# The mixers' small transfers issued by GpSimd instead of SyncE

## The chip, the cores and the metric

The kernel runs on one core of one Trainium2 chip. The metric is the time of one execution in microseconds (us); the median of several runs counts. The engines have short names in what follows: PE is TensorE (matmuls), DVE is VectorE, ACT is ScalarE, POOL is GpSimd and SP is SyncE. SP computes nothing here, it only issues transfers (DMAs). POOL computes and, in this kernel, already issues a few transfers of its own. Each engine works through its own list of instructions strictly in order: an instruction that waits holds back all that stand behind it on that engine.

## The reference

One transformer block over 256 tokens of width 2048, in float32. A norm and one wide projection feed two mixers, a gated delta rule with eight heads and block attention with eight heads. Their outputs go through `w_out`, then 32 experts follow (two of them per token), and a last norm. The part that the change touches is the delta rule's inner matrices:

```python
def gdn_mixer(q, k, v, z, b, a, conv_w, A_log, dt_bias, out_norm_w):
    qkv = jax.nn.silu(causal_depthwise_conv(jnp.concatenate([q, k, v], axis=-1), conv_w))
    ...
    qh = l2norm(heads(q)) * (HEAD_DIM ** -0.5)
    kh = l2norm(heads(k))
    ...
def gated_delta_rule_chunked(q, k, v, g, beta):
    ...
    decay = jnp.exp(jnp.where(causal, g[..., :, None] - g[..., None, :], NEG_INF))
    kb = k * beta[..., None]
    L = jnp.where(strict, jnp.einsum('bhnid,bhnjd->bhnij', kb, k) * decay, 0.0)
    ...
    sol = lax.linalg.triangular_solve(eye + L, rhs, left_side=True, lower=True)
    u, w = sol[..., :Dv], sol[..., Dv:]
    attn = jnp.where(causal, jnp.einsum('bhnid,bhnjd->bhnij', q, k) * decay, 0.0)
```

## The kernel before

**Stages.** The first stage multiplies the normed tokens by `w_in`, 512 columns at a time. Such a block of columns has 16 units; a unit is one slice of 128 rows, whose weights are split into a high part `w_hi` (ACT, line 206) and a low part `w_lo` (DVE, line 208), and 6 or 12 matmuls. SP fetches the weights two units at a time into four buffers (`w_raw`, line 201), and the split runs five units ahead of the matmuls (`SPB = 6` ring tiles). Blocks come in a fixed order: `gk gq gv gz mv` for the first half of the heads, then `gk gq gv mk mq mk gz mq mv`, then four blocks of `w_out`. The second stage is the experts: eight quads of four experts, whose weights SP streams (about 400 MB, line 935) as buffers come free.

**Order of the work.** Everything in the first stage stands in an order written out by hand: the program is a loop over units, and between units a small planner (`tick`, `side_step`) lets generators advance by one step, so the mixers' work is laid between the units. What an engine executes, and in which order, is fixed when the kernel is built; only the waits decide the times. So each transfer stands at one place in its issuing engine's list, and moving it to another engine puts it at the place that the loop had reached on that engine.

**The small transfers.** Heads are done in two halves of four. For each half:

- `decay_task` (once) writes the decay rows to DRAM (`drow`, line 379); `decay` reads them back, each row copied to all 128 partitions, as `E`: two transfers per head (lines 391 and 393, 256 and 128 KB), eight per half. POOL masks them (line 400, four selects per head) and ACT takes exponentials (lines 405 to 407).
- `qk_task` computes the norm factors: POOL takes the power (line 467), PE transposes (470), ACT copies (`rks`, 472), then `drk` goes to DRAM (475) and comes back on all partitions as `RN` (479, four times 256 KB). POOL multiplies `kq` by `RN` (482), and PE forms the products `pA` (488, 493).
- `pA` times `E` goes to DRAM (`dU`, 496) and comes back as blocks of 32 by 32 (`UB`, 515). `inverse` solves them on DVE (lines 520 to 526), sends the inverses to DRAM (`dY`, 529), and `heads` fetches them as `YY` (536). Each head's first matmul on them is `pz` (line 600).

In the kernel before, SP issues all of these, between the weight loads.

Of the kernel before, what the change touches and what calls it, by code (L numbers as in the profile page):

```python
# [40 lines left out]
def bcast_rows(ap, offset, n, parts=128):  # L41
    return bass.AP(tensor=ap.tensor, offset=ap.offset + offset, ap=[[0, parts], [1, n]])
# [3 lines left out]
def tile_block(ctx, tc, x, norm_mix_w, w_in, conv_w, A_log, dt_bias, gonw, monw, w_out, nfw,  # L46
               w_rg, b_rg, w_re, b_re, w_g, w_u, w_d, nfinal, out, dbg=None):
    nc = tc.nc
# [234 lines left out]
    def more_consts():  # L283
        nc.gpsimd.iota(iot, pattern=[[1, SL]], base=1, channel_multiplier=0, allow_small_or_imprecise_dtypes=True)
        nc.gpsimd.iota(dsc, pattern=[[-1, 32]], base=32, channel_multiplier=0, allow_small_or_imprecise_dtypes=True)
        nc.vector.tensor_scalar(tri_le, di, 0.0, None, op0=OP.is_ge)
        nc.vector.tensor_scalar(tri_gt, di, 0.0, None, op0=OP.is_lt)
        nc.vector.tensor_scalar(stri_bf, di, 0.0, None, op0=OP.is_gt)
        nc.vector.memset(ones_bf, 1.0)
        yield  # L290

        dd = wt("cd", [128, 384], "E", EB)
        for c, bs in ((0, 0), (1, 128), (2, 0)):
            nc.gpsimd.iota(dd[:, c * 128:(c + 1) * 128], pattern=[[-1, 128]], base=bs, channel_multiplier=1,
                           allow_small_or_imprecise_dtypes=True)
        for c, bs in ((0, 0), (1, 128), (2, 0)):
            nc.gpsimd.affine_select(out=NEGD[:, c * 128:(c + 1) * 128], in_=dd[:, c * 128:(c + 1) * 128],
                                    pattern=[[-1, 128]], compare_op=OP.is_ge, fill=BIG, base=bs, channel_multiplier=1)
        yield
        nc.vector.tensor_mul(wr, wr, nfr[:, :, None].to_broadcast([128, NK, 36]))  # L300
        yield

        zr = wt("zr", [128, 516], "E", EB)
        nc.vector.memset(zr, 0.0)
        ones = wt("o32", [128, 8, 32], "E", EB)
        nc.vector.memset(ones, 1.0)
        yield
        for i in range(2):
            nc.sync.dma_start(dY.rearrange("c f -> (c f)").rearrange("(a p f) -> p a f", p=128, f=516)[:, i], zr)
        for g in range(4):  # L310
            ps = slice(32 * g, 32 * g + 32)
            nc.gpsimd.affine_select(out=idc[ps], in_=ones[ps], pattern=[[-1, 8], [1, 32]], compare_op=OP.is_equal,
                                    fill=0.0, base=-8 * g, channel_multiplier=0)
# [6 lines left out]
    def decay_task():  # L320
# [55 lines left out]
        rsb = prc.tile([32, 128], F32, name="rsb")  # L376
        nc.scalar.copy(rsb, pr[:32, 0:128])
        yield
        nc.sync.dma_start(drow.rearrange("a h b t -> (a h b) t"), rsb)
        push(decay(0), 3)  # L380

    E = {}
# [1 line left out]
    def decay(hf):  # L384

        heads = range(4 * hf, 4 * hf + 4)
        for H in heads:
            e = wt("E", [128, 6, 128], "E", EB)
            E[H] = e
            off = drow.offset + H * 256  # L390
            nc.sync.dma_start(e[:, 0:4].rearrange("p (a b) t -> p a (b t)", a=2),
                              bass.AP(tensor=drow.tensor, offset=off, ap=[[0, 128], [2048, 2], [1, 256]]))
            nc.sync.dma_start(e[:, 4:6],
                              bass.AP(tensor=drow.tensor, offset=off + 128, ap=[[0, 128], [2048, 2], [1, 128]]))
            yield 1
        yield 1
        for H in heads:
            e = E[H]
            for s, op in ((0, OP.is_gt), (2, OP.is_ge), (4, OP.is_gt), (5, OP.is_ge)):
                nc.gpsimd.affine_select(out=e[:, s], in_=e[:, s], pattern=[[1, 128]], compare_op=op, fill=-BIG, base=0,  # L400
                                        channel_multiplier=-1)
            yield 1
        for H in heads:
            e = E[H]
            nc.scalar.activation(e[:, 0:4:2], e[:, 0:4:2], AF.Exp, bias=negG[:, 0, H:H + 1])
            nc.scalar.activation(e[:, 1:4:2], e[:, 1:4:2], AF.Exp, bias=suf[:, H:H + 1])
            nc.scalar.activation(e[:, 4:6], e[:, 4:6], AF.Exp, bias=negG[:, 1, H:H + 1])
            if H % 2:
                yield 1
# [26 lines left out]
    def qk_task(hf, la, pb):  # L436
# [35 lines left out]
        nc.scalar.copy(rks, prk[:16, 0:128])  # L472
        yield
        drk = drp.tile([16, 128], F32, name=f"drk{hf}")
        nc.sync.dma_start(drk, rks)
        yield
        RN = [wt("RN", [128, 2, T], "YY", 4) for _ in range(4)]
        for h in range(4):
            nc.sync.dma_start(RN[h].rearrange("p a t -> p (a t)"), bcast_rows(drk, h * 512, 512))
        yield  # L480
        for h in range(4):
            nc.gpsimd.tensor_mul(kq[4 * hf + h], kq[4 * hf + h], RN[h])
# [1 line left out]
        for h in range(4):  # L484
            H = 4 * hf + h
            e = E[H]
            p0 = ps_tmp("pA0")
            nc.tensor.matmul(p0, kq[H][:, 0, 0:128], kq[H].rearrange("p a t -> p (a t)"), start=True, stop=True)
            e0 = e[:, 0:4].rearrange("p s t -> p (s t)")
            nc.vector.tensor_mul(e0, p0, e0)  # L490
            p1 = ps_tmp("pA1")
            p1v = p1[:, 0:256].rearrange("p (a t) -> p a t", a=2)
            nc.tensor.matmul(p1v, kq[H][:, 0, 128:256], kq[H][:, :, 128:256], start=True, stop=True)
            nc.vector.tensor_mul(e[:, 4:6], p1v, e[:, 4:6])
            yield 1
            nc.sync.dma_start(square(dU[hf], h), e[:, 0:5:4])
        yield
        side.append(inverse(hf))

# [10 lines left out]
    def inverse(hf):  # L510


        UB = wt("UB", [128, 32, 32], "nat", NATB)
        for g in range(4):
            nc.sync.dma_start(UB[32 * g:32 * g + 32], blocks(dU[hf], 0, 32))
        YB = wt("YB", [128, 8, 32], "YB", 1)
        nc.vector.tensor_copy(YB, idc)
        for _ in range(6):
            yield
        nc.vector.memset(UB.rearrange("p j k -> p (j k)")[:, 0:1024:33], -1.0)  # L520
        for j in range(30, -1, -1):
            n = 32 - j
            pr = wt("ybp", [128, 8, 32], "ybp", 1)[:, :, 0:n]
            nc.vector.tensor_tensor(pr, UB[:, j, None, j:32].to_broadcast([128, 8, n]), YB[:, :, j:32], op=OP.mult)
            yield
            nc.vector.tensor_reduce(YB[:, :, j:j + 1], pr, axis=AX.X, op=OP.add, negate=True)
            yield
        for g in range(4):
            nc.sync.dma_start(blocks(dY, 8 * 128 * g, 8), YB[32 * g:32 * g + 32])
        push(heads(hf), 3)  # L530

    def heads(hf):
        for h in range(4):
            y = wt("YY", [128, 2, 2, 128], "YY", 4)
            YY[4 * hf + h] = y
            nc.sync.dma_start(y[:, 1], square(dY, h))
            push(head_task(4 * hf + h), 5)
            yield 1

# [3 lines left out]
    def square(t, h):  # L543
        return bass.AP(tensor=t.tensor, offset=t.offset + 2 * h * BS, ap=[[128, 128], [BS, 2], [1, 128]])
# [242 lines left out]
    for n in range(16 * 14):  # L787
        kind, hf = chunks[n // 16]
# [617 lines left out]
```

## Time and profile before

| | us |
|---|---|
| median of three runs | 1465.89 (1465.54 to 1466.2) |
| the profiled execution, its own time | 1465.37 |
| its span, first to last instruction | 1463.6 |
| PE busy in the span | 1392.8 |
| DVE, ACT, POOL busy | 623.4, 415.0, 59.8 |

The span is what the profiler records between the first and the last instruction; the execution's own time lies 1.8 us above it. A busy PE is not PE at its peak, since matmuls overlap and their ends are modelled. Waiting, branching and issuing transfers don't count as busy. Of the DMA queues, the one that SP feeds (`q1`) moved 491.93 MB and the one that POOL feeds (`q0`) 0.20 MB.

### The profile page before, as it was taken

What the parts mean: (1) busy time and instruction counts of PE and PEld (TensorE: products, weight loads), DVE (VectorE), ACT (ScalarE), POOL (GpSimd) and SP (SyncE); (2) the same over time, 40 slices, a digit from 0 to 9 for tenths busy, and PEclk for the clock granted to TensorE, in tenths of its full rate; (3) what the DMA queues carried; (4) which work ended last, traced back from release to release, by engine and by line L of the source; (5) the groups of instructions that cost most, each with busy time, mean ns of one, the idle gap of its engine ahead of it and who ended that gap; (6) DMA issues with size and microseconds to landing.
All of it is one profiled execution on the core that took longest, in us unless ns stands there. A gap on an engine that the chain in (4) does not pass through costs nothing.

```text
span 1463.6 us, 19050 instructions
## 1 busy us (share of the span) xinstructions
PE 1392.8 (95%) x7490; PEld 809.9 (55%) x7490; DVE 623.4 (43%) x1287; ACT 415.0 (28%) x806; POOL 59.8 (4%) x93
## 2 busy tenths in 40 slices
PE   8989999999999999999999999999999899899995
PEld 8966999898888844443443443433443334234332
DVE  6846977597655442331331331331151132025024
ACT  5554445555654321120120120111130111003013
POOL 2021003100000000000000000000000000000010
PEclk9999999999999999999999999999999999999998
DMA  8557656765499579999999999999999999999993
GB/s 247 171 167 193 188 174 159 211 182 163 144 359 373 195 285 424 425 419 426 425 414 425 426 426 425 426 424 425 427 427 422 425 425 425 427 426 425 424 403 106
DMA packets 106479, 493.40 MB, mean 337 GB/s; under 512 B 22912, under 2 KB 33248, under 8 KB 77072
## 3 DMA queue, kind: packets, MB, share of 16 engines
q1 hardware_dynamic: 106080, 491.93, 86.5%
q8 instruction: 61, 1.00, 0.3%
q0 software_dynamic: 304, 0.20, 0.1%
q14 instruction: 34, 0.28, 0.1%
HBM read 488.12 MB, written 3.97 MB: 336 GB/s over the span
## 4 chain that ended last, share of the span: by engine, by line
PE 76%; DMA 10%; DVE 5%; issue 4%; ACT 3%; SPq 0%; POOL 0%; ACTq 0%; DVEq 0%; POOLq 0%
PE py L1316 15%; PE pup L1057 13%; PE pgate L1057 12%; PE pj L227 5%; PE pj L228 5%; PE pj L231 5%; DMA we<-in_w_expert_up_dram 4%; PE pj L238 4%; PE pj L241 3%; PE pj L239 3%; PE ph L1046 3%; DMA we<-in_w_expert_down_dram 2%; DMA wm<-in_w_expert_up_dram 2%; DVE acc L1305 2%; ACT xh L1029 2%
## 5 line engine op out<-in xcount | busy, mean ns | idle before, releaser
L208 DVE TENSOR_TENSOR w_lo<-w_raw,w_hi 128x512 fp32r<-128x512 f32 x288 | 197.1, 700 | 115.4 <-ACT w_hi L206 109.4
L206 ACT CAST w_hi<-w_raw 128x512 fp32r<-128x512 f32 x288 | 170.3, 619 | 108.4 <-DMA w_raw<-in_w_in_dram 57.8
L1057 PE MATMUL pup<-we,hT 128*64 128x512 f32 x608 | 165.1, 604 | 7.2 <-DMA we<-in_w_expert_up_dram 7.0
L227 PE MATMUL pj<-xth,w_hi 128*128 128x256 f32 x640 | 165.9, 293 | 0.0
L1316 PE MATMUL py<-we,hgT 128*64 128x512 f32 x544 | 162.9, 597 | 2.1 <-DMA we<-in_w_expert_down_dram 1.4
L228 PE MATMUL pj<-xtl,w_hi 128*128 128x256 f32 x640 | 158.5, 281 | 0.0
L1057 PE MATMUL pgate<-we,hT 128*64 128x512 f32 x528 | 149.1, 600 | 0.0
L227 PEld LDWEIGHTS pj<-xth,w_hi 128*128 128x128 f32 x640 | 121.5, 190 | 1.9 <-ACT w_hi L206 0.4
L228 PEld LDWEIGHTS pj<-xtl,w_hi 128*128 128x128 f32 x640 | 121.8, 190 | 0.2
L1300 DVE SCALAR_TENSOR_TENSOR yl<-py,sl,yh 128x512 fp32r<-128x512 f32 x60 | 43.2, 746 | 175.1 <-ACT yh L1299 174.0
L1035 DVE TENSOR_TENSOR hT<-ph,nfe 128x512 f32<-128x512 f32 x64 | 44.3, 692 | 170.3 <-PE pup L1057 131.6
L1299 ACT ACTIVATE yh<-py,sl 128x512 fp32r<-128x512 f32 x60 | 40.4, 687 | 255.5 <-PE py L1316 227.3
L1283 DVE SCALAR_TENSOR_TENSOR hg<-pup,sl,hg 128x512 f32<-128x512 f32 x16 | 12.0, 751 | 232.2 <-PE pup L1057 224.3
L1057 PEld LDWEIGHTS pup<-we,hT 128*64 128x64 f32 x608 | 51.7, 139 | 99.7 <-issue 88.8
L231 PE MATMUL pj<-xth,w_lo 128*128 128x256 f32 x640 | 101.7, 281 | 0.0
L1029 ACT CAST xh<-xs 128x512 fp32r<-128x512 f32 x64 | 73.7, 1182 | 93.9 <-PE ph L1046 56.8
L1316 PEld LDWEIGHTS py<-we,hgT 128*64 128x64 f32 x544 | 51.8, 136 | 79.1 <-issue 74.1
L1057 PEld LDWEIGHTS pgate<-we,hT 128*64 128x64 f32 x528 | 45.6, 138 | 79.5 <-issue 76.8
L1030 DVE TENSOR_TENSOR xl<-xs,xh 128x512 fp32r<-128x512 f32 x62 | 68.6, 1120 | 49.3 <-PE ph L1046 35.6
L231 PEld LDWEIGHTS pj<-xth,w_lo 128*128 128x128 f32 x640 | 86.9, 190 | 0.0
L1305 DVE TENSOR_TENSOR acc<-acc,pcm 128x512 f32<-128x512 f32 (+1 forms) x122 | 75.3, 674 | 26.3 <-PE pcm L1304 26.2
L1057 PE MATMUL pgate<-wm,hT 128*64 128x512 f32 x256 | 81.1, 595 | 0.0
(329 smaller groups left out, 1981.7 us busy)
## 6 DMA issues: line engine op xcount, KB each, us to landing
we<-in_w_expert_up_dram SPq DMA_DIRECT2D x38, 2048.0 KB, 25.3
we<-in_w_expert_down_dram SPq DMA_DIRECT2D x34, 2048.0 KB, 28.8
we<-in_w_expert_gate_dram SPq DMA_DIRECT2D x33, 2048.0 KB, 22.7
w_raw<-in_w_in_dram SPq DMA_DIRECT2D x111, 512.0 KB, 4.4
wm<-in_w_expert_gate_dram SPq DMA_DIRECT2D x16, 2048.0 KB, 28.3
wx<-in_w_expert_down_dram SPq DMA_DIRECT2D x30, 1024.0 KB, 29.2
wx<-in_w_expert_gate_dram SPq DMA_DIRECT2D x28, 1024.0 KB, 24.4
wx<-in_w_expert_up_dram SPq DMA_DIRECT2D x28, 1024.0 KB, 25.0
```

The source lines that it names most:

```text
L206: nc.scalar.copy(hi, raws[n])
L208: nc.vector.tensor_sub(lo, raws.pop(n), hi.bitcast(F32))
L227: nc.tensor.matmul(o, wh[:, cs], xh[k], start=(k == 0 and c % 2 == 0), stop=False, skip_group_check=True)
L228: nc.tensor.matmul(o, wh[:, cs], xl[k], start=False, stop=False, skip_group_check=True)
L231: nc.tensor.matmul(o, wl[:, cs], xh[k], start=False, stop=(k == NK - 1), skip_group_check=True)
L238: nc.tensor.matmul(pb[b], ah[:, bs], wh, start=(k == 0), stop=False)
L1029: nc.scalar.copy(hi, src)
L1030: engine.tensor_sub(lo, src, hi.bitcast(F32))
L1035: nc.vector.tensor_tensor(hT, ph.rearrange("p (k s) -> p k s", k=2), nfe[:, k0:k0 + 2, None].to_broadcast([128, 2, 4 * SL]), op=OP.mult)
L1057: nc.tensor.matmul(pgu[j * SL:(j + 1) * SL], hT[:, i, c0:c0 + SL], ws[j][kk], start=(half + kk == 0), stop=(half == 1 and kk == 7))
L1305: nc.vector.tensor_add(acc(b, c0, n), acc(b, c0, n) if g + pr else xs[:, b, c0:c0 + n], pc[:, 0:n])
L1316: nc.tensor.matmul(py[c][j * SL:(j + 1) * SL], hgT[pr][:, f, j * SL:(j + 1) * SL], ws[j][f % 2 * 4 + c], start=(f == 0), stop=(f == 3))
```

## The change

Nine `dma_start` calls of the mixers are issued by POOL (`nc.gpsimd`) in place of SP (`nc.sync`). Sizes, shapes, buffers and arithmetic stay, and so do the lists of PE, DVE and ACT.

```diff
--- before.py
+++ after.py
@@ -306,7 +306,7 @@
         nc.vector.memset(ones, 1.0)
         yield
         for i in range(2):
-            nc.sync.dma_start(dY.rearrange("c f -> (c f)").rearrange("(a p f) -> p a f", p=128, f=516)[:, i], zr)
+            nc.gpsimd.dma_start(dY.rearrange("c f -> (c f)").rearrange("(a p f) -> p a f", p=128, f=516)[:, i], zr)
         for g in range(4):
             ps = slice(32 * g, 32 * g + 32)
             nc.gpsimd.affine_select(out=idc[ps], in_=ones[ps], pattern=[[-1, 8], [1, 32]], compare_op=OP.is_equal,
@@ -376,7 +376,7 @@
         rsb = prc.tile([32, 128], F32, name="rsb")
         nc.scalar.copy(rsb, pr[:32, 0:128])
         yield
-        nc.sync.dma_start(drow.rearrange("a h b t -> (a h b) t"), rsb)
+        nc.gpsimd.dma_start(drow.rearrange("a h b t -> (a h b) t"), rsb)
         push(decay(0), 3)
 
     E = {}
@@ -388,9 +388,9 @@
             e = wt("E", [128, 6, 128], "E", EB)
             E[H] = e
             off = drow.offset + H * 256
-            nc.sync.dma_start(e[:, 0:4].rearrange("p (a b) t -> p a (b t)", a=2),
+            nc.gpsimd.dma_start(e[:, 0:4].rearrange("p (a b) t -> p a (b t)", a=2),
                               bass.AP(tensor=drow.tensor, offset=off, ap=[[0, 128], [2048, 2], [1, 256]]))
-            nc.sync.dma_start(e[:, 4:6],
+            nc.gpsimd.dma_start(e[:, 4:6],
                               bass.AP(tensor=drow.tensor, offset=off + 128, ap=[[0, 128], [2048, 2], [1, 128]]))
             yield 1
         yield 1
@@ -472,11 +472,11 @@
         nc.scalar.copy(rks, prk[:16, 0:128])
         yield
         drk = drp.tile([16, 128], F32, name=f"drk{hf}")
-        nc.sync.dma_start(drk, rks)
+        nc.gpsimd.dma_start(drk, rks)
         yield
         RN = [wt("RN", [128, 2, T], "YY", 4) for _ in range(4)]
         for h in range(4):
-            nc.sync.dma_start(RN[h].rearrange("p a t -> p (a t)"), bcast_rows(drk, h * 512, 512))
+            nc.gpsimd.dma_start(RN[h].rearrange("p a t -> p (a t)"), bcast_rows(drk, h * 512, 512))
         yield
         for h in range(4):
             nc.gpsimd.tensor_mul(kq[4 * hf + h], kq[4 * hf + h], RN[h])
@@ -493,7 +493,7 @@
             nc.tensor.matmul(p1v, kq[H][:, 0, 128:256], kq[H][:, :, 128:256], start=True, stop=True)
             nc.vector.tensor_mul(e[:, 4:6], p1v, e[:, 4:6])
             yield 1
-            nc.sync.dma_start(square(dU[hf], h), e[:, 0:5:4])
+            nc.gpsimd.dma_start(square(dU[hf], h), e[:, 0:5:4])
         yield
         side.append(inverse(hf))
 
@@ -512,7 +512,7 @@
 
         UB = wt("UB", [128, 32, 32], "nat", NATB)
         for g in range(4):
-            nc.sync.dma_start(UB[32 * g:32 * g + 32], blocks(dU[hf], 0, 32))
+            nc.gpsimd.dma_start(UB[32 * g:32 * g + 32], blocks(dU[hf], 0, 32))
         YB = wt("YB", [128, 8, 32], "YB", 1)
         nc.vector.tensor_copy(YB, idc)
         for _ in range(6):
@@ -526,14 +526,14 @@
             nc.vector.tensor_reduce(YB[:, :, j:j + 1], pr, axis=AX.X, op=OP.add, negate=True)
             yield
         for g in range(4):
-            nc.sync.dma_start(blocks(dY, 8 * 128 * g, 8), YB[32 * g:32 * g + 32])
+            nc.gpsimd.dma_start(blocks(dY, 8 * 128 * g, 8), YB[32 * g:32 * g + 32])
         push(heads(hf), 3)
 
     def heads(hf):
         for h in range(4):
             y = wt("YY", [128, 2, 2, 128], "YY", 4)
             YY[4 * hf + h] = y
-            nc.sync.dma_start(y[:, 1], square(dY, h))
+            nc.gpsimd.dma_start(y[:, 1], square(dY, h))
             push(head_task(4 * hf + h), 5)
             yield 1
```

On SP, the stretch from the decay rows to the end of the first half's `RN` reads like this before; `w_raw` is a weight load, `drow`, `E`, `drk` and `RN` are the small ones:

```order
L379 DMA drow<-rsb 32x128
L201 DMA w_raw<-in_w_in_dram 128x2x512
L391 DMA E<-drow 128x2x256
L393 DMA E<-drow 128x2x128
L201 DMA w_raw<-in_w_in_dram 128x2x512
```

and after the change, from the last of the early small loads (`nfe`, `brow`) on:

```order
L138 DMA nfe<-in_norm_ffn_w_dram 128x2x8
L139 DMA brow<-in_b_router_group_dram 128x4
L140 DMA brow<-in_b_router_expert_dram 128x32
L201 DMA w_raw<-in_w_in_dram 128x2x512 x103
L201 DMA w_raw<-in_w_out_dram 128x2x512 x5
```

All the small transfers are gone from between the weight loads: 103 of them follow one another.

On POOL, the second half of the heads, from the first half's last power (`so`) to the second half's `kq` products, before:

```order
L646 TENSOR_TENSOR so<-so,mhalf 128x2 x4
L467 TENSOR_TENSOR rk<-rk,mhalf 128x16
L400 AFFINE_SELECT E<-E 128x128 x16
L482 TENSOR_TENSOR kq<-kq,RN 128x512 x4
L741 TENSOR_TENSOR mso<-mso,mhalf 128x2 x4
```

and after, from the last of the four pairs of `E` transfers on (the other three pairs stand right ahead of it, behind the power of line 467):

```order
L391 DMA E<-drow 128x2x256
L393 DMA E<-drow 128x2x128
L475 DMA drk_3290<-rks 16x128
L400 AFFINE_SELECT E<-E 128x128 x8
L479 DMA RN<-drk_3290 128x512 x4
L400 AFFINE_SELECT E<-E 128x128 x8
L482 TENSOR_TENSOR kq<-kq,RN 128x512 x4
```

The eight transfers of `E` now stand on POOL behind the power of line 467, `drk` behind the last of them, and `RN` behind half of the selects; on SP they stood in a list of their own, with no POOL instruction ahead of them.

On POOL, the same half's inversion, before and after (`mso` is the attention's norm, `so` the delta rule's):

```order
L741 TENSOR_TENSOR mso<-mso,mhalf 128x2 x4
L646 TENSOR_TENSOR so<-so,mhalf 128x2 x4
```

```order
L496 DMA dU_142<-E 128x2x128 x4
L515 DMA UB<-dU_142 32x32x32 x4
L741 TENSOR_TENSOR mso<-mso,mhalf 128x2 x3
L529 DMA dY<-YB 32x8x32 x4
L741 TENSOR_TENSOR mso<-mso,mhalf 128x2
L536 DMA YY<-dY 128x2x128 x4
L646 TENSOR_TENSOR so<-so,mhalf 128x2 x4
```

The sends and returns of the blocks now lie among POOL's few powers.

## Rows read from the trace of the kernel before

**Rows 1.** The page's head: span of the profiled execution.

```profile
span 1463.6 us, 19050 instructions
```

**Rows 2.** Windows: length, busy us (instructions) per engine, PE clock, DMA share, GB/s.

```profile
92.00:120.00 28.00, 17.76 (x69) 11.67 (x69) 18.25 (x34) 15.95 (x32) 12.46 (x17) 1.00 0.62 194
120.00:124.00 4.00, 4.00 (x10) 2.47 (x11) 3.38 (x6) 2.02 (x7) 0.00 (x0) 0.57 0.50 133
490.00:500.00 10.00, 10.00 (x50) 8.38 (x50) 4.67 (x7) 4.38 (x8) 0.00 (x0) 1.00 0.45 157
1402.00:1406.00 4.00, 4.00 (x17) 1.49 (x15) 0.00 (x0) 0.00 (x0) 2.52 (x4) 1.00 1.03 430
```

**Rows 3.** Waits of PE, 50 to 500 us: total us, times, longest us.

```profile
PE pj L238 <- ACT w_hi L206: 4.1, 3, 1.4
PE pj L241 <- DVE w_lo L208: 3.5, 3, 2.1
```

**Rows 4.** Timeline of SP, first half: start us, us, engine, line, transfer.

```profile
70.97 0.33 SPq L379 DMA_DIRECT2D drow<-rsb  x1
...
87.79 7.46 SPq L201 DMA_DIRECT2D w_raw<-in_w_in_dram  x4
```

**Rows 5.** Timeline of PE, first half's first pA and first pz.

```profile
120.45 1.05 PE L488 MATMUL pA<-kq 128*128 128x512 f32 x1
...
195.20 0.32 PE L600 MATMUL pz<-YY,E 32*32 32x32 f32 x8
```

**Rows 6.** Page section 6: DMA issues, count, KB each, us from issue to landing.

```profile
dY<-YB SPq DMA_DIRECT2D x8, 32.0 KB, 1.7
...
fnb<-in_norm_final_w_dram POOLq DMA_DIRECT2D x4, 2.0 KB, 5.6
...
r<-in_gdn_out_norm_w_dram POOLq DMA_DIRECT2D x1, 0.5 KB, 5.4
```

**Rows 7.** Timeline of POOL, start of the program.

```profile
2.29 0.52 POOL L116 DMA_DIRECT2D r<-in_gdn_out_norm_w_dram  x1
```

**Rows 8.** Timeline of SP: first send of YB, then the second half.

```profile
186.01 1.81 SPq L529 DMA_DIRECT2D dY<-YB  x4
...
233.80 0.51 SPq L391 DMA_DIRECT2D E<-drow  x1
...
257.48 1.76 SPq L479 DMA_DIRECT2D RN<-drk  x4
```

**Rows 9.** Timeline of POOL, second half; idle before and its releaser in brackets.

```profile
242.28 3.21 POOL L467 TENSOR_TENSOR rk<-rk,mhalf 128x16 f32<-128x16 f32 x1 [4.37 <-DVE rk L465]
245.46 3.77 POOL L400 TENSOR_SCALAR_AFFINE_SELECT E<-E 128x128 f32<-128x128 f32 x8
...
256.02 0.54 POOL L400 TENSOR_SCALAR_AFFINE_SELECT E<-E 128x128 f32<-128x128 f32 x2 [0.87 <-DMA E<-drow]
260.80 3.74 POOL L482 TENSOR_TENSOR kq<-kq,RN 128x512 f32<-128x512 f32 x3 [4.24 <-DMA RN<-drk]
265.31 1.27 POOL L482 TENSOR_TENSOR kq<-kq,RN 128x512 f32<-128x512 f32 x1 [0.77 <-DMA RN<-drk]
```

**Rows 10.** Timeline of VectorE: beside POOL's products, and at UB's arrival.

```profile
112.42 3.37 DVE L208 TENSOR_TENSOR w_lo<-w_raw,w_hi 128x512 fp32r<-128x512 f32 x2
...
142.61 0.09 DVE L520 MEMSET UB<- 128x32 f32 x1 [2.94 <-DMA UB<-dU]
```

**Rows 11.** Timeline of PE, second half's first two pA and first pz.

```profile
262.33 1.02 PE L488 MATMUL pA<-kq 128*128 128x512 f32 x2
...
267.47 1.10 PE L488 MATMUL pA<-kq 128*128 128x512 f32 x2 [1.41 <-ACT bv L565]
...
345.11 0.32 PE L600 MATMUL pz<-YY,E 32*32 32x32 f32 x8
```

**Rows 12.** Timeline of SP, second send of YB.

```profile
334.41 1.81 SPq L529 DMA_DIRECT2D dY<-YB  x4
```

**Rows 13.** Page section 5: the split on VectorE; count, busy us, mean ns.

```profile
L208 DVE TENSOR_TENSOR w_lo<-w_raw,w_hi 128x512 fp32r<-128x512 f32 x288 | 197.1, 700 | 115.4 <-ACT w_hi L206 109.4
```

## The prediction

> **What bounds the kernel now.** I read the page's head first: the span is 1463.6 us [rows 1], and the profiled execution took 1465.37, so 1.8 us lie around it; the sum below is made against 1465.37, which is 0.5 under the median. Next the windows. Between 490 and 500 us, at the end of the first stage, the DMA engines are only 0.45 busy [rows 2]: all buffers open to expert weights are filled by then. Late in the expert stage, at 1402 to 1406, they are full, 1.03 at 430 GB/s [rows 2]. The second stage therefore runs at the rate of its weight stream and starts from the same filled buffers whenever the first stage ends. I take what the first stage gains or loses one to one to the end.
>
> In the first stage PE is the bound, and the windows show where it is not fed: of 28 us between 92 and 120 it is busy 17.76, so 10.2 are idle, and right behind that it runs 4 us at a mean granted clock of 0.57, part of them at 1.2 GHz [rows 2]. The waits of PE name the releasers: the split weights, 4.1 and 3.5 us [rows 3]. SP's timeline says why they are late: four weight loads go out only at 87.79, behind the transfers of E [rows 4]. This is what the change removes.
>
> **What it removes.** SP's list becomes weight loads alone, and they go out as buffers come free. The first half's idle 10.2 us are the most that this can give, plus 1.7 for the slow clock (4 us at 0.57). What is late next is the first product `pA`, at 120.45 [rows 5], whose operands now hang on POOL's own chain.
>
> **What a hop costs on POOL.** A tiny transfer of SP lands 1.7 us after its issue; POOL's tiny ones take 5.4 at the start and 5.6 at the end [rows 6], the latter with the DMA engines full. I take 5.5 for a hop issued by POOL, and 1.7 as the other end, in case the rows owe their length to the start and the full engines. One issue occupies POOL for 0.52 us [rows 7].
>
> The Trainium skill, in DMA: Bandwidth & Descriptors, section Latency and other measured facts, gives about 1 us to the first byte for a transfer issued by GpSimd and about 0.6 from the other path. By it a hop would grow by an estimated 0.4 us rather than 3.8; the rows here disagree as they stand, and rival D works out what a short hop would do.
>
> **What the broadcast of E costs on POOL.** No row shows it. On SP the second half's eight transfers took from 233.80 to 256.0 [rows 8, 9], 22.2 us, with two weight loads between them. Shortest end: RN, also copied to 128 partitions, moved its 1 MB from 257.48 to 265.3 [rows 8, 9], 7.8 us, so 1.5 MB would take 11.7. Longest end: eight weight loads beside it in place of two, six more of 0.5 MB at 430 GB/s [rows 2], 1.2 us each, give 29.7 (an estimate). POOL issues the eight back to back, so SP's pauses go: I take 20, nearer to the row than to either end. That transfers of two queues share the engines rather than line up is shown by the 5.6 us of `fnb` beside a full stream.
>
> **First half.** `drow` is sent at 70.97 [rows 4] and lands at 76.5; E has landed by 96.5; the last head's four selects (two take 0.54 [rows 9]) end at 97.6. `drk` stands behind them on POOL, so it lands at 103.1, RN at 108.6, and the first `kq` product, a third of 3.74 [rows 9], is ready at 109.9. `pA` could start 10.6 us earlier than at 120.45; the ceiling is 10.2: **-10.2**. With E at 29.7 it is -0.9, at 11.7 still -10.2. Of the slow clock I count half back, **-0.9**, since short stalls stay.
>
> The same half's inverses: SP sends `YB` from 186.01 [rows 8]. On POOL the fourth send goes out at 187.6, lands at 193.1, and the first `YY` lands at 198.6, where PE wants it at 195.20 [rows 5]: **+3.4**. With hops of 1.7 there is no stall. The trip through `dU` and `UB` also grows, by at most twice 3.8, 7.6 us. Its cover: DVE stood 2.94 us before `UB` came at 142.61 [rows 10], and no wait of PE came of it, as the split runs five units ahead; 50 matmuls in 10 us, six a unit [rows 2], make a unit at least 1.2 us, so the cover is 6. I count nothing; without cover it costs what is over, up to 1.6 us in each half, and more if UB is later still.
>
> **Second half.** Here the order on POOL works against the change. SP could send E from 233.80, ahead of all else. Now the eight stand behind the power of line 467, which waits for DVE and ends at 245.5 [rows 9]. E then lands at 265.5. `drk` stands behind E in the same queue and lands no earlier; RN lands at 271.0. Between them POOL has eight selects (four RN issues end at 267.6, 3.77 us of selects at 271.4), so the first product is ready at 272.6, where `pA` started at 262.33 [rows 11]: 10.3 late. Before the second `pA`, at 267.47, PE waited 1.4 us on ACT, which the later start swallows: **+8.9**. With E at 29.7 it is +18.6; at 11.7 the first product is ready at 264.0, and 0.3 is left. Queued behind the waiting `pA` are the weight matmuls of that stretch, so all of PE stands. After a stall of that length I expect the clock to dip as it did at 120, **+1.7**.
>
> The second send of `YB` starts at 334.41 [rows 12]: on POOL the fourth goes out at 336.0, `YY` is there at 347.0 and wanted at 345.11 [rows 11]: **+1.9**; nothing with short hops.
>
> Other parts at nothing: clearing `dY` near 30 us adds two issues, 1.0 us, to POOL ahead of line 160; no weight is late there, and uncovered it costs 1.0. SP's shorter list frees nothing after 350 us.
>
> **Sum:** -10.2 - 0.9 + 3.4 + 8.9 + 1.7 + 1.9 = +4.8, so 1465.37 + 4.8 = **1470.2 us**.
>
> **The rivals.**
>
> *A, the forecast.* Gain in the first half, a little more than that lost behind POOL's order and its hops. With E between 17 and 24 us the time goes from 1467 to 1478.
>
> *B, faster: the broadcast runs like RN.* On a queue of its own E takes 11.7 us. Then the second half loses next to nothing at `pA`, no clock dips, and the sum is -10.2 - 1.7 + 0.3 + 3.4 + 1.9 = -6.3: 1459. It decides below about 15 us of E. For it: RN's rate. Against it: E's rows are shorter (1 KB and 512 bytes instead of 2 KB), and the weights now run beside it.
>
> *D, short hops.* With hops of 1.7 both `YY` terms vanish. The second half stays late, because the selects between `drk` and RN's products end at 271.4 whatever the hop: -10.2 - 0.9 + 8.9 + 1.7 = -0.5: 1465, no change that can be measured. For it: SP's 1.7. Against it: both POOL rows.
>
> *C, POOL is kept from issuing by DVE.* Beside POOL's products two splits took 3.37 us [rows 10], where one takes 0.7 on the mean [rows 13]: the two engines hold each other up. If every issue waits out one 0.7 us operation of DVE, E's eight take 5.6 more and each later hop 0.7: the first half gives -3.6, the second +14.9, the `YY` stalls 6.9 and 5.4, the clock 1.7, together +25.3: 1491. Against it: the 3.37 is a case of two inputs read by both, which an issue is not.
>
> The Trainium skill, in SBUF — State Buffer, section SBUF: two separate sides, states such a rule: while VectorE runs in a two-port mode GpSimd cannot write its descriptors, and it advises against transfers from GpSimd beside such work. No run here shows a POOL transfer beside a busy DVE, so the trace neither agrees nor disagrees yet.
>
> *That the change does nothing* I rule out: SP's list loses every small transfer.
>
> **How the numbers follow.** Chances: A 0.47, B 0.27, D 0.16, C 0.10. A measurement of this kernel can tell about 0.2% from no change, 2.9 us either way of 1465.89: below 1463.0 is faster, above 1468.8 slower. Faster: 0.25 of B and 0.04 of D, 0.29. Same: 0.05 of A (the end near 1467), 0.02 of B, 0.10 of D, 0.17. Slower: 0.42 of A, 0.02 of D, all of C, 0.54. The predicted time is A's, 1470.2; A's own range is 1467 to 1478. The range for 8 in 10 goes from 1458 to 1482: it takes in B down to its centre and leaves out B's fast end (0.10) and most of C (0.09).
>
> **What would show it.** In the windows of the changed kernel: 92 to 120 without idle 10 us; PE idle of 8 to 12 us in one piece where the second half's first `pA` stands, released by POOL's `kq` product; two waits of 2 to 4 us at `pz`, released by `YY`. In the issues: POOL's `dY` landing near 5.5 us, E's eight within 20. I am wrong if `pA` in the second half is not late (B), if `dY` lands in 2 us (D), or if POOL's issues stretch beside DVE (C).

## The result, and the profile after

| | before | after |
|---|---|---|
| median, us (runs) | 1465.72 (6) | 1478.82 (6, 1475.94 to 1481.98) |
| profiled execution / its span | 1465.37 / 1463.6 | 1481.98 / 1480.2 |
| mean granted clock | 0.989 | 0.981 |

The changed kernel is slower by 13.1 us; the ratio is 1.0092, interval [1.0079, 1.0104]. The forecast was slower by 4.8. The profiled execution is the slowest of the six, 3.2 us over the median.

The windows of the changed kernel (span us, length, then busy us of PE, PEld, DVE, ACT, POOL with counts, granted clock, DMA share, GB/s):

```profile
92.00:96.00 4.00, 0.13 (x1) 0.00 (x0) 0.00 (x0) 0.00 (x0) 0.00 (x0) 0.90 0.48 145
92.00:120.00 28.00, 19.08 (x68) 14.32 (x67) 19.30 (x34) 15.83 (x32) 14.33 (x22) 0.80 0.54 166
120.00:124.00 4.00, 3.94 (x9) 2.43 (x9) 3.25 (x7) 1.91 (x5) 0.00 (x0) 0.50 0.62 157
...
265.00:278.00 13.00, 0.00 (x0) 0.00 (x0) 0.66 (x1) 2.98 (x9) 5.30 (x13) 0.67 0.64 188
```

Two things are to be seen against [rows 2]. In the first half nothing is won: PE is idle 8.9 us of 92 to 120 in place of 10.2, now with all engines still from 92 to 96, and the clock is lower. In the second half PE stands still for 13 us in one piece. PE's waits name both:

```profile
PE pA L488 <- POOL kq L482: 13.2, 1, 13.2
PE pj L238 <- ACT w_hi L206: 4.6, 1, 4.6
...
PE pj L241 <- DVE w_lo L208: 3.3, 2, 3.0
```

The waits for split weights of [rows 3] are still there, 4.6 and 3.3 us; the 13.2 us are new. The timeline of POOL at that place tells how they come about (start, length, then the idle time before and what ended it):

```profile
244.78 3.21 POOL L467 TENSOR_TENSOR rk<-rk,mhalf 128x16 f32<-128x16 f32 x1 [4.37 <-DVE rk L465]
247.95 0.75 POOL L391 DMA_DIRECT2D E<-drow  x1
...
253.02 0.72 POOL L393 DMA_DIRECT2D E<-drow  x1
255.39 0.53 POOL L475 DMA_DIRECT2D drk<-rks  x1 [1.65 <-ACT vT L431]
...
272.69 2.20 POOL L479 DMA_DIRECT2D RN<-drk  x4 [8.81 <-DMA drk<-rks]
274.90 1.99 POOL L400 TENSOR_SCALAR_AFFINE_SELECT E<-E 128x128 f32<-128x128 f32 x8
276.87 4.94 POOL L482 TENSOR_TENSOR kq<-kq,RN 128x512 f32<-128x512 f32 x4
```

SP sent E from 233.80 [rows 8]; POOL sends it from 247.95, behind the power of line 467. The last transfer of E, sent at 253.02, took 19.2 us and landed at 272.2; `drk`, sent behind it, landed at 272.4. Then come RN, selects and products, and `pA` starts at 278.18, where it was 262.33 [rows 11].

The difference between the two traces, place by place: first `pA` of the first half +0.6 us (121.08 against 120.45), line 467 of the second half +2.5, `pA` of the second half +15.9, first stage's end (line 1078) +16.0, span +16.6. So the second half lost 13.4, and what the first stage lost went to the end nearly one to one. The 1.9 us between the first `pA` and line 467 are mostly a slower clock right behind `pA` (1.3 us by the first `pz`) and 0.6 us in which `pz` waited for `YY`. The clock in 124 to 128, changed kernel first, then the kernel before:

```profile
124.00:128.00 4.00, 4.00 (x15) 2.95 (x14) 1.70 (x4) 1.13 (x3) 0.78 (x1) 0.76 0.55 164
```

```profile
124.00:128.00 4.00, 4.00 (x18) 2.94 (x18) 1.85 (x4) 1.95 (x6) 0.00 (x0) 1.00 0.11 33
```

### The profile page after: what moved, and what is told of

Its sections match the earlier page's. It is cut to its first block, busy times and chain, and to the rows that moved or that the text cites. A ratio compares the mean times of both kernels' runs of the same rounds, so it can differ in the third digit from the quotient of the medians.

```text
span 1480.2 us, 19057 instructions
## 1 busy us (share of the span) xinstructions
PE 1396.2 (94%) x7490; PEld 817.8 (55%) x7490; DVE 625.3 (42%) x1287; ACT 416.1 (28%) x806; POOL 98.3 (7%) x154
## 4 chain that ended last, share of the span: by engine, by line
PE 70%; DMA 14%; DVE 6%; issue 6%; ACT 2%; POOL 2%; SPq 0%; ACTq 0%; POOLq 0%; DVEq 0%
PE py L1316 15%; PE pgate L1057 12%; PE pup L1057 12%; PE pj L227 4%; PE pj L231 4%; DMA we<-in_w_expert_up_dram 4%; PE pj L228 4%; PE pj L238 3%; PE pj L241 3%; PE pj L239 3%; PE ph L1046 3%; DMA we<-in_w_expert_down_dram 2%; DMA wm<-in_w_expert_up_dram 2%; DVE acc L1305 2%; DMA we<-in_w_expert_gate_dram 2%
## 5 line engine op out<-in xcount | busy, mean ns | idle before, releaser
L1299 ACT ACTIVATE yh<-py,sl 128x512 fp32r<-128x512 f32 x60 | 40.4, 687 | 255.8 <-PE py L1316 227.6
L1057 PE MATMUL pgate<-wm,hT 128*64 128x512 f32 x256 | 81.1, 596 | 0.0
```

The source lines that it names most:

```text
L1057: nc.tensor.matmul(pgu[j * SL:(j + 1) * SL], hT[:, i, c0:c0 + SL], ws[j][kk], start=(half + kk == 0), stop=(half == 1 and kk == 7))
```

## The experiments

Medians in us; the ratio is to the kernel before on the same chip, with its 95% interval.

| run | what differs | median | ratio |
|---|---|---|---|
| `e_on_sp` | changed kernel, E on SP | 1470.20 | 1.0037 [1.0024, 1.0050] |
| `e2_on_sp` | changed kernel, E on SP in the second half | 1467.63 | 1.0024 [1.0016, 1.0033] |
| `only_e` | before, E alone on POOL | 1473.10 | 1.0054 [1.0041, 1.0066] |
| `rk_pool` | before, drk and RN alone on POOL | 1467.17 | 1.0014 [1.0006, 1.0023] |
| `late_pow4` | changed kernel, line 467 behind six sends of E | 1467.81 | 1.0019 [1.0008, 1.0030] |
| `rep8` | changed kernel, drow eight times | 1478.00 | 1.0093 [1.0080, 1.0106] |
| `lean_sp` | before, without line 393 | 1452.32 | 0.9912 [0.9899, 0.9925] |
| `fat_sp` | before, without line 393, E in pieces of 2 KB | 1452.55 | 0.9919 [0.9906, 0.9932] |
| `fat_pool` | `fat_sp` with the change | 1456.54 | 0.9945 [0.9932, 0.9958] |
| `fat_inv` | `fat_sp`, inversion's transfers on POOL | 1454.99 | 0.9935 [0.9922, 0.9948] |

**Which part loses: E back on SP, in both halves and in one.**

```diff
-            nc.gpsimd.dma_start(e[:, 0:4].rearrange(...
+            nc.sync.dma_start(e[:, 0:4].rearrange(...
```
(the same in line 393; in the second kernel `(nc.sync if hf else nc.gpsimd)`)

> The changed kernel with the eight transfers of E per half (lines 391 and 393) issued by SP again; drow, drk, RN, dU, UB, dY and YY stay on POOL. Theory 1 (the loss is E on POOL's list: in the second half it stands behind line 467 and drk behind it; the inverse chain's hops cost next to nothing): the second half's first pA starts within 3 us of the kernel before, the time is 1464 to 1468, no change against before, 11 to 15 us faster than the changed kernel. Theory 2 (POOL's hops and its work as an issuer cost, whatever stands on its list): most of the 13 us stays, 1474 to 1478.

> The changed kernel with E issued by SP in the second half only; in the first half E stays on POOL. Theory 1 (the first half neither gains nor loses by the change, all of the loss is the second half's E on POOL): 1465 to 1469, and the first pA of the first half within 2 us of 120.45. Theory 3 (the first half loses too, through its longer stretches of slow clock at 96 to 128 us): 1469 to 1473.

With E on SP in both halves 0.55% of the 0.92% are gone, with E on SP in the second half 0.68%. So most of the loss is E in the second half, and E on POOL in the first half costs nothing: its first `pA` stands at 120.2 in `e2_on_sp`. Neither run came back to the kernel before, though: the first misses both ranges. Of the +4.9 us of span of `e_on_sp` 1.3 are there at the first `pA`, 2.1 at `pz`, 3.0 at the second half's `pA`.

**E alone on POOL.**

```diff
-            nc.sync.dma_start(e[:, 0:4].rearrange(...
+            nc.gpsimd.dma_start(e[:, 0:4].rearrange(...
```
(the same in line 393)

> The kernel before with only E's transfers on POOL; drk and RN go on SP, so they don't stand behind E in one queue. Theory 1a (POOL's list sets the end: the products of line 482 stand behind the selects of line 400, and these wait for E, which goes out only after line 467): the second half's pA is still late by 12 to 16 us and the time is 1475 to 1480. Theory 1b (drk and RN stuck behind E in POOL's queue set the end): pA comes some 6 to 9 us earlier than in the changed kernel and the time is 1468 to 1473.

By `pA` it is theory 1b: it starts at 269.8, 8.4 us earlier than in the changed kernel, and waits 8.2 us for POOL's product in place of 13.2; the median lies 0.1 us above the range of 1b. SP sends `drk` at 246.9, among POOL's sends of E; it lands at 255.8, with the transfer of E sent at 246.0 (256.0) and ahead of the one sent at 246.8 (257.9). In the changed kernel it goes out at 255.4, after all of E, and lands after all of E. The kernel before has both on SP, and `rk_pool` below has `drk` on POOL and E on SP: there it goes out at 248.5 and 248.2, behind the last send of E, and lands at 257.5 and 257.8, with E's last (256.0 and 257.9). So in all four it is the moment of sending that decides, not the queue, and POOL's order delays `drk` as well as E.

**drk and RN alone on POOL.** Lines 475 and 479 get `nc.gpsimd`, nothing else.

> The kernel before with only drk and RN (lines 475 and 479) on POOL. It tells where the 6 us come from that the changed kernel with E on SP still loses. Theory 5 (RN's four issues and landings on POOL stand between the selects and the products, some 2 us in each half): 1466 to 1469, pA about 1.5 us late in the first half and 2 to 3 in the second. Theory 6 (the inversion's transfers on POOL cost it): the time of the kernel before within 1.5 us.

Theory 5: `pA` is 1.4 us late in the first half and 2.7 in the second, the span 1.7 longer. That is part of what `e_on_sp` left over; the rest, some 3 us, is not settled.

**The place on POOL's list.** The power moves four steps later in the second half, and the wait behind it is dropped, so that PE's transpose keeps its place:

```diff
+        if hf:
+            yield 4
         nc.gpsimd.tensor_tensor(rkf, rkf, mhalf, op=OP.pow)
-        yield 4
+        if hf < 1 or 4 < 4:
+            yield 4-4*hf
```

> The changed kernel; only on POOL, and only in the second half, the power of line 467 moves behind six of E's eight sends. The lists of PE, DVE, ACT and SP stay as they are. Theory 1 (E is late because it stands behind line 467, which waits for DVE): E's first send goes out right behind the four powers of line 646, near 240.5 instead of 247.95, E lands and pA starts 6 to 8 us earlier than in the changed kernel; the time is 1470 to 1473. Theory 4 (the lateness is the broadcast's own slowness from POOL, not its place on the list): pA gains under 2 us, 1476 to 1479.

POOL in this kernel (line 467 is 469 here):

```profile
235.50 1.00 POOL L649 TENSOR_TENSOR so<-so,mhalf 128x2 f32<-128x2 f32 x1 [2.12 <-DVE so L648]
236.45 0.75 POOL L391 DMA_DIRECT2D E<-drow  x1
...
240.82 3.29 POOL L469 TENSOR_TENSOR rk<-rk,mhalf 128x16 f32<-128x16 f32 x1
244.06 0.76 POOL L391 DMA_DIRECT2D E<-drow  x1
244.82 0.72 POOL L393 DMA_DIRECT2D E<-drow  x1
246.77 0.53 POOL L478 DMA_DIRECT2D drk<-rks  x1 [1.23 <-ACT rks L475]
...
257.78 2.18 POOL L482 DMA_DIRECT2D RN<-drk  x4 [6.65 <-DMA drk<-rks]
```

The first send goes out 11.5 us earlier, the last lands at 257.3 in place of 272.2, `pA` starts at 265.5 and no longer waits for POOL. One instruction in another place takes back 0.73 of the 0.92%, some 10.7 us, more than expected. That most of the loss is the place on POOL's list is shown. Not all of the 14.9 us by which E's last landing is earlier is the earlier start, though: E also took 20.9 us here (236.45 to 257.3) and 24.3 in the changed kernel.

**Why the first half won nothing: the broadcast itself.** In the changed kernel SP sent weights at 77.5 and 81.1; the answer for the first of these sends:

```profile
L201 SPq DMA_DIRECT2D w_raw<-in_w_in_dram x1: 368/368/368, 77.5 to 77.5; - x1
...
DMA to landing us min/median/max: 18.5/18.5/18.5
```

It landed at 96.0, with the transfers of E that POOL sent at 78.0 and 78.7 (94.8 and 96.1). In the kernel before the weights sent at 81.3 landed at 92.7, also among those of E sent just ahead and behind (90.9, 96.2). The load did not stand in a line as a whole. From 84.3, where the load ahead of it landed, to 96.0 the two queues moved (packets, MB, share of the 16 engines; SP feeds q1, POOL q0):

```profile
q1 hardware_dynamic: 872, 1.69, 40.6%
q0 software_dynamic: 278, 0.81, 38.7%
```

So over three loads' worth of SP's bytes went through beside E, and no load landed: a load counts when its last piece is there, and that came with the end of E. Which piece lags, and why, the traces don't tell. So a shorter E, still on SP, was tried:

```diff
-            nc.sync.dma_start(e[:, 4:6], ...)
...
-            for s, op in ((0, OP.is_gt), (2, OP.is_ge), (4, OP.is_gt), (5, OP.is_ge)):
-                nc.gpsimd.affine_select(out=e[:, s], in_=e[:, s],
+            for s, r, op in ((0, 0, OP.is_gt), (2, 2, OP.is_ge), (4, 1, OP.is_gt), (5, 3, OP.is_ge)):
+                nc.gpsimd.affine_select(out=e[:, s], in_=e[:, r],
```

> The kernel before, all on SP, without the second transfer of E per head (line 393): the selects for slots 4 and 5 read slots 1 and 3, which hold the same values, so nothing else is left out. Half of E's descriptors and a third of its bytes go. Theory 1 (the broadcast itself takes the time and holds up the weights beside it, whichever queue issues it): E takes 11 to 15 us in place of 22, weights and the second half's pA come 4 to 9 us earlier each, the time is 1452 to 1462. Theory 2 (SP's list order holds the weights up, one issue after another): four SP issues fewer per half give back some 3 us, 1461 to 1465.

It is 0.88% faster than the kernel before. E has landed by 85.7 instead of 97.3, the first `pA` starts 10.5 us earlier (109.93), and the window and the only weight wait left in the first half are

```profile
92.00:120.00 28.00, 25.89 (x104) 19.09 (x104) 20.68 (x35) 16.01 (x38) 8.89 (x14) 0.94 0.52 158
```

```profile
PE pj L241 <- DVE w_lo L208: 2.1, 1, 2.1
```

The second half's own stretch is unchanged (line 467 to `pA`: 20.2 against 20.1), so the whole gain is the first half's. The changed kernel took E off SP's list and kept its traffic, and won nothing here; this run keeps E on SP and has a third less of its bytes. So the idle 10 us were E's traffic, not SP's order.

**The change with a cheap broadcast.** `drow` laid out by head, so that one transfer of 2 KB pieces brings a head's E; then the change on top of it, and the inversion's part alone:

```diff
-    drow = drp.tile([2, 8, 2, 128], F32, name="drow")
+    drow = drp.tile([8, 2, 2, 128], F32, name="drow")
...
+            nc.sync.dma_start(e[:, 0:4].rearrange("p s t -> p (s t)"), bcast_rows(drow, H * 512, 512))
```

> The kernel before, all on SP, with drow laid out by head, so that one transfer per head brings the four rows of E as pieces of 2 KB (128 of them, in place of 256 of 1 KB and 256 of 512 bytes); slots 4 and 5 are selected from slots 1 and 3. The bytes are those of the lean kernel (1452.3), the pieces half as many. Theory N (number of pieces): E's four transfers take some 8 us where the lean kernel's took 12.7 (72.9 to 85.6), first pA 1 to 3 us earlier than its 109.9, 1449 to 1452. Theory B (bytes): E takes 12 to 13 us and the time is that of the lean kernel within 1.5 us.

> The change under study (all nine calls on POOL) on top of the kernel with E in pieces of 2 KB, so to be compared with that kernel on SP. Theory 1 (the change loses because the slow broadcast of E stands on POOL behind line 467 with drk behind it): with a cheap broadcast it loses much less, 2 to 6 us over its partner on SP, 1452 to 1457. Theory 2 (POOL's hops and issues cost whatever E takes): it still loses 11 to 15 us over its partner, 1462 to 1466.

> The kernel with E in pieces of 2 KB on SP, with only the inversion's transfers on POOL: clearing dY, dU, UB, YB to dY, and YY. Theory 1 (these hops cost next to nothing on POOL, and SP's weights gain nothing by their leaving): the time of its partner with all on SP within 2 us. Theory 3 (each hop of POOL is some 2 us longer, and E, with the changed kernel on SP, lost 6 us by it): 3 to 6 us slower than its partner.

`fat_sp` takes the time of `lean_sp`: by the time it is theory B, larger pieces of the same bytes give nothing. E itself was a little shorter, 10.9 us in the first half and 12.6 in the second, against 12.7 and 13.2 in `lean_sp`. On top of `fat_sp` the change (`fat_pool`) loses 0.26%, some 4 us, where it lost 0.92%: theory 1. The intervals of the two just touch. The profiled execution of `fat_pool` is the fastest of its runs; in it E lands 8.2 us later than in `fat_sp` (243.2 against 235.0) and the second half's `pA` is only 0.6 us late, so the trace doesn't show where the others lose. One of its six executions took 3558.74 us, more than twice the rest, and is not in the ratio; what happened there is not known. `fat_inv` loses 0.16% with overlapping intervals, which lies between its two theories: not settled.

**Why E is slow.** First the copies in DRAM:

```diff
-    drow = drp.tile([2, 8, 2, 128], F32, name="drow")
+    drow = drp.tile([8, 2, 8, 2, 128], F32, name="drow")
...
-    ap=[[0, 128], [2048, 2], [1, 256]]
+    ap=[[0, 16], [4096, 8], [2048, 2], [1, 256]]
```

> The changed kernel, with drow written eight times over in DRAM by one transfer, and each transfer of E reading the copies in turn, so that a DRAM row is read by 16 partitions instead of 128. Number and size of E's pieces stay (256 of 1 KB and 256 of 512 bytes per head). Theory H (E is slow because all partitions read the same DRAM addresses): E's eight transfers take under 12 us, the weights beside them land within 6 us, the second half's pA is 8 to 12 us earlier than in the changed kernel, the time 1460 to 1470. Theory N (E is slow by the number and smallness of its pieces): E still takes 22 to 26 us and the time is 1476 to 1483, with one longer hop for the eightfold drow.

In the second half E took 22.7 us, and the time is that of the changed kernel. By that run theory H falls. The next two, which run groups of transfers by themselves, show that this was too quick. Both send their groups ahead of everything else, the groups read here with nothing beside them; each transfer waits for the one four places ahead of it, so that the sends come at the pace of the landings.

```diff
+    group(nc.sync, 0, True, 256)      # one DRAM row for all partitions
+    group(nc.sync, 0, True, 128)
...
+    group(nc.sync, nw, True, 256)     # a row of its own for each
```

> The kernel before with seven groups of four transfers ahead of everything else, each group waiting for the one before, nothing beside them; its time is not to be compared. SP: (1) 128 copies of two pieces of 1 KB, (2) of two pieces of 512 bytes, (3) of one piece of 2 KB, (4) and (5) as 1 and 2 but each partition from its own DRAM row; POOL: (6) as 1, (7) as 3. Theory N (time goes by the number of pieces): (1) and (2) take about the same, 9 to 12 us, (3) about half, (4) as (1). Theory H (the shared DRAM address): (4) under half of (1). Theory W (E is slow only because weights run beside it): every group under 6 us.

Windows inside groups 1 to 5 (SP) and then 6 (POOL), of which the DMA share and GB/s at the end of each row count:

```profile
4.00:8.00 4.00, 0.00 (x0) 0.00 (x0) 0.00 (x0) 0.00 (x0) 0.00 (x0) 1.00 0.48 160
11.00:15.00 4.00, 0.00 (x0) 0.00 (x0) 0.00 (x0) 0.00 (x0) 0.00 (x0) 1.00 0.24 73
18.00:20.00 2.00, 0.00 (x0) 0.00 (x0) 0.00 (x0) 0.00 (x0) 0.00 (x0) 1.00 0.44 170
22.00:24.00 2.00, 0.00 (x0) 0.00 (x0) 0.00 (x0) 0.00 (x0) 0.00 (x0) 1.00 0.95 309
24.50:26.50 2.00, 0.00 (x0) 0.00 (x0) 0.00 (x0) 0.00 (x0) 0.08 (x1) 1.00 0.77 205
31.00:35.00 4.00, 0.00 (x0) 0.00 (x0) 0.00 (x0) 0.00 (x0) 1.17 (x3) 1.00 0.90 153
```

One shared row: 160 GB/s, 1.6 us for the larger transfer of a head; half the bytes in pieces of 512 bytes run at 73 GB/s and so take 1.8 us, no less; pieces of 2 KB run at 170. Rows of their own: 309 GB/s with pieces of 1 KB, 205 with 512 bytes. Theory N was right that groups 1 and 2 take about the same, but its halving for 2 KB falls; theory W falls too (a group of 1 KB pieces from one row takes over 6 us even alone), and H is right by a factor of two to three. That is not all of E's time: at these rates E's eight transfers would take an estimated 13.7 us alone (four at 1.6, four at 1.8), and beside the weights they took 22 to 24. In the second half of the changed kernel SP's queue moved 2.33 MB in those 24.3 us, an estimated 5.4 us at 430 GB/s [rows 2]; some 5 us stay open.

The second probe varies the copies:

```diff
+    group([[0, 16], [4096, 8]])       # eight rows 16 KB apart, in turn
+    group([[0, 16], [nw, 8]])         # eight rows 28 KB apart, in turn
+    group([[nw, 8], [0, 16]])         # eight rows, blocks of 16 partitions
```

> The kernel before with transfers ahead of everything else, all of 128 pieces of 2 KB (256 KB); its time is not to be compared. First seven groups of four on SP, whose source is one DRAM row for all partitions; eight rows 16 KB apart in turn; eight rows 26 KB apart in turn; eight rows, each for 16 neighbouring partitions; 16 rows in blocks of eight; 32 rows in blocks of four; a row of its own for each. Then three rounds in which four loads of 256 KB from rows of their own go out on SP while a broadcast from one row runs on POOL, while the same amount from rows of their own runs on POOL, and while a broadcast from one row runs on SP. Theory H (partitions that read one address at the same moment hold each other up; copies in turn don't help, since neighbours move in step, copies in blocks do): one row and eight in turn take 1.5 to 1.8 us for each 256 KB, blocks 0.6 to 1.0, own rows 0.7. Theory H2 (any eight copies help, and the eightfold copy failed for another reason): eight in turn under 1.0 too. For the loads beside the broadcast: theory F (what is in flight goes through the engines in order, whichever queue sent it): the loads land 3 to 7 us later beside POOL's broadcast than beside POOL's own rows. Theory S (queues share the engines evenly): under 2 us later.

Windows inside these three groups, in this order:

```profile
10.00:14.00 4.00, 0.00 (x0) 0.00 (x0) 0.00 (x0) 0.00 (x0) 0.00 (x0) 1.00 0.63 175
14.00:16.00 2.00, 0.00 (x0) 0.00 (x0) 0.00 (x0) 0.00 (x0) 0.00 (x0) 1.00 0.90 303
18.00:22.00 4.00, 0.00 (x0) 0.00 (x0) 0.00 (x0) 0.00 (x0) 0.00 (x0) 1.00 0.52 164
```

Copies 16 KB apart, which `rep8` used, run like one row; copies one row of w_in apart (28 KB; the 26 in the expectation was a slip), read in turn, run at almost twice that; in blocks of 16 partitions they don't help (by the sends, a group took 5.9, 3.6 and 7.0 us; blocks of eight and of four partitions 3.5 and 4.0). So `rep8` did not test what it was meant to, and both theories had the layout wrong. Loads beside a broadcast were also tried there; the trace gives no landing for them, so the order of landings rests on the traces of the kernels above.

## Why the prediction was right in direction and short in size

The measured 1478.8 lies inside the range of 1458 to 1482 and 0.8 above the forecast's own 1467 to 1478 (A). In the profiled execution, 16.6 us slower, the first half up to its first `pz` gives +1.9 where the sum had -11.1, the two `YY` terms about +0.8 where it had +5.3, and the second half with its clock 13.4 where it had 10.6. The errors go both ways, so that the sum was off by no more is in part luck.

- **"What it removes" failed.** The step was that SP's weights go out as buffers come free and then arrive: -10.2. The sends did move ahead (77.5, 81.1, 82.7 and 86.9, where SP before sent at 81.3 and then from 87.79 [rows 4]), but the weights landed when E was through, from 96.0 on. The claim under it, that transfers of two queues share the engines rather than line up, was drawn from a 2 KB row (`fnb`). It holds for the bytes (1.69 MB of SP's beside 0.81 of POOL's), but not for the landing of a 512 KB load, and the split waits for the landing. Measured +0.6 in the profiled execution. The ceiling was right: `lean_sp` wins 10.5 at that place. Its reading was not quite: the weights are 7.6 of the idle 10.2, and 2.6 are PE waiting for POOL's power (line 467). The kernel before:

```profile
PE prk L470 <- POOL rk L467: 2.6, 1, 2.6
```

- **E in the first half, 20: near, by luck.** The prediction had E land at 96.5, after a 5.5 us hop of `drow`; it landed at 96.1, after a hop of 1.7 and 22.4 us of broadcast.
- **The slow clock, -0.9, failed with it.** The clock was 0.80 in 92 to 120 (1.00 before), 0.50 in 120 to 124 (0.57) and 0.76 in 124 to 128 (1.00).
- **Second half, +8.9: mechanism right, size short.** Line 467 ends where the prediction put it (247.95, less the 2.5 that came from earlier), PE waits in one piece for POOL's product, and `late_pow4` proves the place on the list. At `pA` the forecast was 10.3 us late (8.9 is what is left when the 1.4 us wait for ACT is taken off); it was 13.4, so 3.1 are missing. The mis-sized term is E: 24.3 us instead of 20, 4.3 more. From E's last landing to `pA` it took 6.0 us instead of 7.1, since the eight selects took 1.99 and not 3.77. The pauses that were taken off for POOL's back-to-back sends gave nothing in this half (24.3 against 22.2 on SP). The long end of E, 29.7, is a slip: 22.2 and six times 1.22 make 29.5.
- **YY, +3.4 and +1.9: too large.** A small hop on POOL in the middle of the program is not 5.5 us. The changed kernel's issue rows (KB each, median us from send to landing), and behind them that of `YY` in the kernel before:

```profile
E<-drow POOLq DMA_DIRECT2D x8, 256.0 KB, 13.1
...
YY<-dY POOLq DMA_DIRECT2D x8, 128.0 KB, 5.1
...
dY<-YB POOLq DMA_DIRECT2D x8, 32.0 KB, 3.2
...
drow<-rsb POOLq DMA_DIRECT2D x1, 16.0 KB, 1.7
```

```profile
YY<-dY SPq DMA_DIRECT2D x8, 128.0 KB, 5.5
```

  `dY` took 3.2 (SP 1.7 [rows 6]), `drow` 1.7, and `YY` 5.1, no more than on SP; `pz` waited 0.6 in all. Rival D was nearer on the hop, and wrong on the first half like A.
- **The clock after the stall, +1.7: the dip came, net nothing is left of it.** After 13 us without work PE ran 4 us at 0.50, that is at 1.2 GHz:

```profile
278.00:282.00 4.00, 3.82 (x10) 2.62 (x11) 3.48 (x1) 3.58 (x9) 3.81 (x4) 0.50 0.00 1
```

  That is an estimated 2.0 us. But from `pA` to the second half's first `pz` it is 83.0 us, and was 82.8: about as much as the 2.0 us that PE before waited for ACT in that stretch, 1.4 of which the forecast had taken off already.
- **Rival C fell.** In 245 to 255 DVE was busy 9.96 of 10 us, and POOL sent E's eight transfers in it at 0.72 to 0.75 each; with DVE idle, sends of the same shape took 0.72 to 0.73 behind a first of 1.02 in the first probe.

```profile
245.00:255.00 10.00, 10.00 (x88) 9.99 (x87) 9.96 (x23) 5.19 (x11) 8.74 (x9) 1.00 0.83 143
```

  The rule of the Trainium skill that the prediction names (SBUF — State Buffer, section SBUF: two separate sides) speaks of VectorE in a two-port mode. Which mode the operations of this stretch used no trace shows, so the rule is neither confirmed nor refuted; no cost is seen.
- **Rival B fell** with E's 24 us: RN was not the model for it. Half of E's transfers come in pieces of 512 bytes and RN's all in 2 KB; by the probe's rates E would take an estimated 13.7 us alone, where RN's rate gave 11.7. Most of the rest came beside the weights, as said above, and some 5 us of it stay open.

The failed gain and the missing 3.1 us both go back to one unmeasured thing, the broadcast. The Trainium skill has a rule that would have helped with the first: DMA: Bandwidth & Descriptors, section Issuing engines are not separate DMA queues, says that transfers of all issuing engines run on the same 16 DMA engines, so spreading them over issuers only saves issue time. The bytes and the landings of weights and E from 84.3 to 96.0 agree.

## What to carry to other kernels

Before moving a transfer to another issuer, read what stands ahead of it on that engine's list, and whether the victim waits for the send or for the landing: here the sends got through and the landings did not. A transfer that all partitions read from one DRAM row is worth shortening first; dropping E's duplicate transfers (half of their number, a third of the bytes) won 0.88%, and the change that moved E with the other small transfers lost 0.92%. What is in flight ahead counts, whichever engine sent it.

## What the runs showed of the hardware

- Reading one DRAM row into 128 partitions runs at 153 to 170 GB/s alone in pieces of 1 or 2 KB, rows of their own at 309 in pieces of 1 KB; at 512 bytes a piece it is 73 against 205. Eight copies read in turn help 28 KB apart (303) and not 16 KB apart (175). The Trainium skill, in DMA: Bandwidth & Descriptors, section Latency and other measured facts, tells of slow DRAM copies at large power-of-two row pitches, cured by a few KiB of padding; these runs may show the same at a far smaller pitch, but that is not shown: the two pitches differ in size too, and at 28 KB blocks of 16 partitions were as slow (164).
- The DMA share does not tell the rate of a broadcast: in pieces of 1 KB it is 0.48 when SP sends it and 0.90 when POOL does, at 160 and 153 GB/s; in pieces of 2 KB SP's shows 0.44 in one probe and 0.79 in the other, at 170 and 165 GB/s.
- Around the broadcasts transfers landed in the order in which they were sent, across SP's and POOL's queues, to within 1.2 us in the changed kernel, 2.4 in `only_e` and `late_pow4` and 3.8 once in `e_on_sp`. Their bytes moved side by side.
